# Recurrent slots, first down products and sixteen residual stores put in another order, in a decoder layer on one core

## The chip, the core and the metric

The kernel runs on one core of one Trainium2 chip. The core has TensorE (PE: matmuls, and PEld: the loads of their weights), VectorE (DVE), ScalarE (ACT), GpSimd (POOL), SyncE (SP, which here only gives out transfers) and 16 DMA engines that all transfers share. The metric is the device time of one execution in microseconds (us). Three runs of the kernel before took 1535.04, 1535.98 and 1536.03 us, so the median is 1535.98 us.

## The reference

One decoder layer over 1024 positions of 1024 channels in float32: RMSNorm, one input projection, two branches side by side, an output projection and a residual, and then an MLP with a residual and a last RMSNorm.

```python
h = rms_norm(x, g_mix)
z = h @ w_in + b_in                      # six parts: 1024, 1024, 1536, 1536, 1024, 1024 wide
# branch A: gated linear unit, causal width-31 depthwise conv, layer_norm, silu, @ w_a_out
# branch B: causal width-4 depthwise conv, then the gated recurrence:
r = sigmoid(block_diag(v, w_rg_a));  i = sigmoid(block_diag(v, w_rg_x))   # 16 heads of 96
a = exp(-8 * r * softplus(-lam));    h_t = a_t * h_{t-1} + sqrt(1 - a_t^2) * i_t * v_t
x = x + (sigmoid gates of both branches, merged) @ w_o
x = x + relu(rms_norm(x, g_mlp) @ w_1) ** 2 @ w_2
out = rms_norm(x, g_final)
```

## The kernel before

**Numbers.** A product in float32 is made of three products in a rounded format: each operand is split in a high and a low half, and high by high, high by low and low by high are added up in PSUM. So nearly every operand is followed by a split: ACT makes the high half by a copy, and the low half is the operand minus it. Either DVE subtracts (`low`, L1211), or ACT writes the negated high half, a POOL transfer adds the operand on top of it, and ACT copies (`split_dma`, L63 to L67). The large products (output projection, up and down projection) are block products of the Strassen kind, so that operands are sums of blocks (`d_sum`, L1866 to L1889) and results are added up block by block.

**Slots.** The input projection and the recurrence run as slots, `for s in range(3, NC1)` (L807 on). A slot is one 128-channel chunk of `z`, 48 matmuls (`chunk_mm(s, 0, 12)` and `chunk_mm(s, 12, 24)`, lines L723), with one head of the recurrence between or after them. A head has two products, one for each gate, of six matmuls (`head_mm`, L532 to L534), both in a PSUM bank that exists once. `head_gate` (sigmoid on ACT, L542) empties that bank. `head_mm(n, 0)` stands at the end of head n's slot and `head_mm(n, 1)` behind the first twelve pairs of the next one. Four heads make a group of three 128-channel tiles. One slot after a group's last head comes its `scan_exp` (L551 to L557: an exp and a tanh per tile on ACT), one more slot later its `scan_root`, and `scan_in` (the multiplication L462 of the gate `g` by the conv output `v`, on DVE) and `scan_tile` come in between. `EXP` maps these slots to the groups: {8: 0, 13: 1, 18: 2, 22: 3}. A tile `v` is made by an ACT pass and three conv taps (L474, L483), and `xb_parts` splits it into `vth` and `vtl` for the head (L488, with `split_dma`).

In these slots the order on every engine is written out. DVE's order is made by a small planner: `clk` holds an estimated time for each engine, `later(ready, cost, f)` puts work into a list with the time from which it can run, `vector_work(until)` gives that list out in order of those times and fills what is left of DVE's estimated time up to `until` with taps of the width-31 conv. `begun` is the planner's time for PE at the slot's start, `clk["P"]` its running time for PE.

**Output projection and residual.** The residual `x1` is made transposed (channels on partitions). `x1_turn` (L1528 on) turns half of it back with DVE transposes into four tiles `x1r` and stores each with four transfers into `x1d` in DRAM (L1539): 16 stores of 128 KB. These stand in the part in which SP's order too is written out. The other half goes through PE transposes (`x1_rows`, L1571). The down projection reads `x1d` back as `xb` (L2013).

**Up projection.** 104 steps (`useq`, L1942 on) of 12 matmuls each. Here the order on PE, ACT and DVE is written out. SP's and POOL's isn't: a scheduler places their transfers in the build. `UX` (L1843) maps a step number to additional calls.

**Down projection.** Four groups g of seven products p with two halves kk; `m` counts the 14 steps of a group (loop L2119 to L2165). In a step the operands of the next two steps are split (`left_high` on ACT L1904, `right` on ACT L1915; both return the low half as a function that is called later, DVE L1211), the block sums for later steps are made (`d_sum`), and two half products run on PE (`down_mm`, L1987). After the second half kk = 1 the results are taken over: the first half at once, the second (`down_add(g, p, 1)`) is held and given out at the start of the next step. For p = 1 that is an ACT copy `d0b<-d0a` (L2001), upon which p = 2 goes on adding in the bank `d0a`; for p = 2 it is a DVE addition into `xb` (L2005). In the steps called `joint` the low halves and the sums go out together after the first half product.

Tiles of [128, 1024] live in one pool of 37 buffers for the whole kernel, so a new tile can have to wait until a store of an old one has been read.

Of the kernel before, what the change touches and what calls it, by code (L numbers as in the profile page):

```python
# [15 lines left out]
P = 128  # L16
# [14 lines left out]
def trunk_kernel(ctx: ExitStack, tc: tile.TileContext, x, xt_in, xt_eo, vecs, w_in, w_a_out, w_b_pl, w_b_sq,  # L31
# [457 lines left out]
    def xb_parts(t):  # L489
        vp_[t] = T(f"vth{t}", F32R), T(f"vtl{t}", F32R)  # L490
        split_dma(vt[t], *vp_[t])
        parts[4 * (t // 3) + t % 3] = vp_[t]
        at("A", 2.1)
# [17 lines left out]
    def head_w(n):  # L511
        raw = rp.tile([HD, 2, HD], F32, tag="rraw", name=f"rraw{n}")
        nc.sync.dma_start(raw, w_rg[n])
        gws[n] = raw
# [33 lines left out]

    at_, rooted = {}, {}

    def scan_exp(g):  # L551
        at("A", 1.28)
        for t in range(3 * g, 3 * g + 3):
            r = gate[0, t]
            at_[t] = T(f"a{t}")
            nc.scalar.activation(at_[t], r, AF.Exp, scale=c8[:, t:t + 1])
            nc.scalar.activation(r, r, AF.Tanh, scale=c4[:, t:t + 1])  # L557
            at("A", 2.2)
# [8 lines left out]
    def scan_in(ready, *ts):  # L567
        for t in ts:
            later(ready, 1.2, nc.vector.tensor_tensor, gate[1, t], gate[1, t], vt.pop(t), ALU.mult)
# [144 lines left out]
    def chunk_mm(s, n0, n1, halves=(0, 1)):  # L714

        wh, wl = wst[s]
        if s not in zps:
            zps[s] = PS(f"z{s}")
        pairs = [x for k in range(8) for x in ((wh, k, 0), (wh, k, 1))] + [(wl, k, 0) for k in range(8)]
        for n in range(n0, n1):  # L720
            w, k, part = pairs[n]
            for hf in halves:
                nc.tensor.matmul(zps[s][:, HALVES[hf]], w[:, k, :], xw[k][part][hf],  # L723
                                 start=n == 0, stop=n == 23)
        at("P", len(halves) * (n1 - n0) * MM)
# [81 lines left out]
    with tc.manual_schedule(engines=ENGINES):  # L807
        for s in range(3, NC1):
            w_load(s + 2)
            for t in sorted(vp_):  # L810
                head_load(t)
            taps["hold"] = False
            begun = clk["P"]
            clk["A"], clk["V"] = max(clk["A"], begun + 0.5), max(clk["V"], begun - 2)

            if s == 3:

                chunk_mm(s, 0, 24, (1,))
                rs = first_scale()
                first_product(0, rs)  # L820
                xb_out(0, zps[0])
                first_parts(rs)
                chunk_mm(s, 0, 24, (0,))
            else:
                chunk_mm(s, 0, 12)
            before, new, nxt = (head_at.get(s + d) for d in (-1, 0, 1))
            if before is not None:

                head_gate(before, 0, begun)
                head_mm(before, 1)  # L830
            if made:
                xb_parts(made.pop())
            if s > 3:
                chunk_mm(s, 12, 24)
            if new is not None:
                head_mm(new, 0)

            c = CH[s - 1]
            if c >= XB:
                xb_out(c - XB, zps[s - 1])  # L840
            elif c >= GA:
                if CH[s] == c - GA + VA:
                    u_gate(c - GA, zps[s - 1])
                else:
                    u_out(c - GA, zps[s - 2], zps[s - 1])
            w_parts(s + 1)
            if before is not None:
                head_gate(before, 1, clk["P"] - 30 * MM)
            if s - 1 in EXP:

                scan_root(EXP[s - 1])
            if s == 3 or c >= XB:
                made.append(0 if s == 3 else c - XB)
            if nxt is not None:
                head_w_parts(nxt)
            if s == 5:
                decay_on()
            if s + 2 in head_at:
                head_w(head_at[s + 2])
            for d in range(5):  # L860
                if s - d in EXP:
                    g = EXP[s - d]
                    if d == 0:
                        scan_exp(g)
                        scan_in(begun + 3.5, 3 * g, 3 * g + 1)
                    elif d == 1:
                        scan_in(begun + 3.5, 3 * g + 2)

                    t = 3 * g + d - (2 if g < 3 else 1)
                    if 3 * g <= t < 3 * g + 3:  # L870
                        later(rooted[t], 4.8, scan_tile, t)
            if s == NC1 - 1:
                z_get(0, z_lhs)
                z_get(1, z_lhs)
            for f, *a in XS.get(s, ()):
                f(*a)
            if s == NC1 - 3:
                for i in range(4):
                    z_load(i // 2, i % 2)
            if s == 3:  # L880
                for c2 in range(4):
                    nc.sync.dma_start(xu[0, c2], xc[c2])
            vector_work(clk["P"] - 0.7)
# [646 lines left out]
    def x1_turn(kk):  # L1530
        for th in range(2):
            r = T(f"x1r{kk}{th}")
            for c2 in range(2):
                src = x1[kk, 0, c2].rearrange("p (m h b j) -> p h m b j", m=2, h=2, j=32)[:, th]
                dst = r.rearrange("p (b m j) -> p m b j", m=4, j=32)[:, 2 * c2:2 * c2 + 2]
                dve(0.65, 0, nc.vector.transpose, dst, src)
            d = x1d[2 * th:2 * th + 2].rearrange("q (b i) (k g x) -> k g i (q b) x", b=4, k=2, g=4)
            for g in range(4):
                nc.sync.dma_start(d[kk, g], r[32 * g:32 * g + 32].rearrange("p (b x) -> p b x", x=P))  # L1539

    def x1_cols():

# [271 lines left out]
    with tc.manual_schedule(engines=ENGINES):  # L1814
# [9 lines left out]
        for n in range(len(gseq) + 1):  # L1824
# [18 lines left out]
    UX = {0: ((g_parts, "u", 7, 0), (g_t, "u", 0, 4)), 1: ((g_parts, "u", 7, 1), (g_t, "u", 1, 4)),  # L1843
          2: ((g_parts, "u", 3, 0),), 3: ((g_parts, "u", 3, 1),), 4: ((g_parts, "u", 4, 0),),
          5: ((g_parts, "u", 4, 1),)}
    KC = 4
    NC_ = NP // KC
    BLK = {11: 0, 22: 1, 21: 2, 12: 3}
# [269 lines left out]
    with tc.manual_schedule(engines={mybir.EngineType.Activation, mybir.EngineType.DVE,  # L2118
                                     mybir.EngineType.PE}):  # L2119
        for n, (g, p, kk) in enumerate(dseq[:-2]):  # L2120
            m = n % 14
            end = g == NC_ - 1
            nx, nx2 = dseq[n + 1], dseq[n + 2]
            if m in DLOADS and not end:
                d_load(g + 1, *DLOADS[m])
            elif m == 0:
                d_load(g, *DFIRST)
            if n == 0:
                for q2 in range(2):
                    acc[0, 0, q2] = x_block(0, 0, q2)  # L2130
            if (g, m) in XADD:
                xbs[g, m] = x_block(*XADD[g, m])
            if held:
                held.pop()()
            lows_ = []
            if not end or m < 10:
                lows_.append(left_high(*nx))
            sums_ = d_sums(g, m)
            joint = not g and m in (2, 3)
            if sums_ and not joint:  # L2140
                d_sum(*sums_.pop(0))
            if not end or m < 10:
                lows_.append(right(*nx2))
            down_mm(g, p, kk, 0)
            if joint:
                for f in lows_:
                    f()
                for x in sums_[::-1]:
                    d_sum(*x)
            if kk:  # L2150
                if end and p == 7:
                    d_last(0)
                else:
                    down_add(g, p, 0)
            if not joint:
                for f in lows_:
                    f()
                for x in sums_:
                    d_sum(*x)
            if (g, m - 4) in XADD:  # L2160
                k = XADD[g, m - 4]
                tt(acc[k], acc[k], xbs.pop((g, m - 4)), ALU.add)
            down_mm(g, p, kk, 1)
            if kk:
                held = [lambda g=g, p=p: down_add(g, p, 1)]  # L2165
            if end:
                for f, *a in FX.get(m, ()):
                    f(*a)
        d_group(du["f", 0], z, 4, 0, (0, 1), False, True)
        d_last(1)  # L2170
        out_sq(1, 1, 0)
        out_sq(1, 1, 1)
        out_pre(1, 1, 1)
        close(0)
        d_group(du["f", 1], z, 4, P, (0, 1), False, True)
        closed(0)
        close(1)
        d_group(du["f", 2], z, 4, 2 * P, (0, 1), False, True)
        closed(1)
        close(2)  # L2180
        d_group(du["f", 3], z, 4, 3 * P, (0, 1), False, True)
        close(3)
        closed(2)
        closed(3)
# [80 lines left out]
```

## Time and profile before

| | |
|---|---|
| median of three runs | 1535.98 us |
| the profiled execution | 1536.15 us |
| its span, first to last instruction | 1534.1 us |
| outside the span | 2.05 us |
| granted TensorE clock, mean | 0.998 |
| busy: PE, DVE, ACT, POOL | 1521.0, 1199.6, 929.3, 192.3 us |
| HBM read, written | 149.79 MB, 60.82 MB |

The span is the time between the first and the last instruction of the profiled execution. A busy time is the sum of the engine's instructions. PE is busy for 99% of the span, so the kernel is a row of matmuls with few pauses, and 13.1 us lie in the pauses. In lists of single instructions the first column is the start in us from the span's begin, the second the duration, and brackets at the end give the idle time before it and what released it. Matmuls overlap in their pipeline: one of 128x512 shows as 0.39 us, yet the next one starts 0.23 us later.

### The profile page before, as it was taken

The numbers are of one execution on the slowest core, as the hardware profiler recorded it, in microseconds if no ns is written. First come the engines' busy times: TensorE is split into PE (matmuls) and PEld (weight loads), VectorE is DVE, ScalarE is ACT, GpSimd is POOL, SyncE is SP. The second block draws the span as 40 slices with busy tenths as digits, with TensorE's granted clock in tenths as the row PEclk, the third lists the DMA queues.
The fourth block names the chain that finished last, engine by engine and source line by source line (L and its number), as shares of the span: only waits on it lengthen the run. The fifth ranks groups of instructions, "written<-read, shape, count | busy, mean of one in ns | idle before, by whom it ended". The sixth has DMA issues, their size and how long they took to land.

```text
span 1534.1 us, 18971 instructions
## 1 busy us (share of the span) xinstructions
PE 1521.0 (99%) x6722; PEld 1250.4 (82%) x6722; DVE 1199.6 (78%) x1636; ACT 929.3 (61%) x1299; POOL 192.3 (13%) x228
## 2 busy tenths in 40 slices
PE   9999999999999999999999999999999999999998
PEld 7877877788888888888888887888888888888886
DVE  6989897899999997788769889755555386777777
ACT  6748678586566656735475877554444445545475
POOL 0111011012222222000022322000000000101010
PEclk9999999999999999999999999999999999999999
DMA  9766778898997889864779898333333974776465
GB/s 350 189 145 148 181 157 174 220 258 199 270 261 177 197 207 253 295 234 116 268 199 302 194 192 211 137 117 113 113 111 111 298 265 128 171 217 167 110 123 153
DMA packets 130799, 296.53 MB, mean 193 GB/s; under 512 B 12896, under 2 KB 34912, under 8 KB 130704
## 3 DMA queue, kind: packets, MB, share of 16 engines
q1 hardware_dynamic: 98960, 215.92, 41.9%
q0 software_dynamic: 31600, 79.15, 28.1%
q8 instruction: 52, 0.85, 0.2%
q14 instruction: 43, 0.35, 0.1%
q10 hardware_dynamic: 144, 0.26, 0.0%
HBM read 149.79 MB, written 60.82 MB: 137 GB/s over the span
## 4 chain that ended last, share of the span: by engine, by line
PE 86%; issue 5%; DVE 4%; DMA 3%; POOL 1%; ACT 1%; SPq 0%; POOLq 0%; DVEq 0%
PE z L723 12%; PE d1b L1987 2%; PE d2b L1987 2%; PE d0b L1987 2%; PE d3b L1987 2%; PE d0e L1987 1%; PE d3e L1987 1%; PE d3a L1987 1%; PE d2e L1987 1%; PE d2a L1987 1%; PE d1e L1987 1%; PE d1a L1987 1%; PE z L258 1%; DVE v L483 1%; DVE y L635 1%
## 5 line engine op out<-in xcount | busy, mean ns | idle before, releaser
L723 PE MATMUL z<-xh,win_h 128*128 128x512 f32 x368 | 115.4, 391 | 0.0
L723 PE MATMUL z<-xl,win_h 128*128 128x512 f32 x368 | 114.9, 390 | 0.0
L635 DVE SCALAR_TENSOR_TENSOR y<-u,vec,y 128x511 f32<-128x511 f32 (+14 forms) x120 | 88.5, 737 | 0.0
L723 PE MATMUL z<-xh,win_l 128*128 128x512 f32 x368 | 87.4, 389 | 0.0
L635 DVE SCALAR_TENSOR_TENSOR yt<-u,vec,yt 128x511 f32<-128x511 f32 (+6 forms) x112 | 82.6, 738 | 0.0
L635 DVE SCALAR_TENSOR_TENSOR y<-yt,csum,y 128x511 f32<-128x511 f32 (+6 forms) x112 | 82.6, 738 | 0.0
L723 PEld LDWEIGHTS z<-xh,win_h 128*128 128x128 f32 x368 | 69.1, 188 | 16.1 <-ACT win_h L67 0.5
L723 PEld LDWEIGHTS z<-xl,win_h 128*128 128x128 f32 x368 | 69.1, 188 | 15.0
L723 PEld LDWEIGHTS z<-xh,win_l 128*128 128x128 f32 x368 | 69.1, 188 | 14.5
L542 ACT ACTIVATE g<-rg,vec 96x1024 f32<-96x1024 f32 x32 | 35.5, 1110 | 65.3 <-PE rg L534 65.1
L1683 ACT ACTIVATE o<-s 128x512 fp32r<-128x512 f32 x56 | 33.7, 623 | 45.7 <-DVE s L1667 26.4
L66 POOL DMA_DIRECT2D zo<-zw x45 | 39.2, 871 | 134.4 <-ACT zo L65 122.8
L483 DVE SCALAR_TENSOR_TENSOR v<-xb,vec,v 128x1023 f32<-128x1023 f32 (+2 forms) x36 | 46.1, 1280 | 2.6 <-ACT v L474 1.8
L66 POOL DMA_DIRECT2D db_10l<-br x4 | 3.5, 876 | 340.5 <-ACT db_10l L65 340.5
L65 ACT ACTIVATE zo<-zw 128x512 fp32r<-128x512 f32 x45 | 28.2, 626 | 24.2 <-PE z2f L921 2.1
L66 POOL DMA_DIRECT2D win_l<-win_raw x23 | 20.0, 868 | 179.7 <-ACT win_l L65 151.1
L1211 DVE TENSOR_TENSOR o<-s,o 128x512 fp32r<-128x512 f32 x56 | 37.3, 684 | 1.4 <-ACT o L1683 1.4
L66 POOL DMA_DIRECT2D zo<-zs x30 | 26.4, 879 | 75.7 <-ACT zo L65 63.6
L462 DVE TENSOR_TENSOR g<-g,v 128x1024 f32<-128x1024 f32 x12 | 14.3, 1220 | 23.3 <-DMA g<-g 23.3
L67 ACT ACTIVATE zo<-zw 128x512 fp32r<-128x512 f32 x45 | 27.9, 621 | 0.0
L576 DVE TENSOR_TENSOR_SCAN g<-a,g 128x1024 f32<-128x1024 f32 x12 | 27.5, 2292 | 0.4
L66 POOL DMA_DIRECT2D ga<-gsa x8 | 7.0, 874 | 161.0 <-ACT ga L65 158.8
(3182 smaller groups left out, 4925.1 us busy)
## 6 DMA issues: line engine op xcount, KB each, us to landing
w_raw<-in_w_dram SPq DMA_DIRECT2D x34, 512.0 KB, 5.5
br<-in_w_dram SPq DMA_DIRECT2D x32, 512.0 KB, 5.9
ar<-fd SPq DMA_DIRECT2D x32, 512.0 KB, 6.9
zw<-in_w_in_dram SPq DMA_DIRECT2D x28, 512.0 KB, 6.9
win_raw<-in_w_in_dram SPq DMA_DIRECT2D x23, 512.0 KB, 5.0
win_l<-win_raw POOLq DMA_DIRECT2D x23, 512.0 KB, 5.1
zo<-zw POOLq DMA_DIRECT2D x45, 256.0 KB, 5.5
gates<-zg SPq DMA_DIRECT2D x32, 256.0 KB, 4.2
```

What stands on the lines that cost most here:

```text
L65: nc.scalar.activation(l, src, AF.Copy, scale=-1.0)
L66: nc.gpsimd.dma_start(l, src, accum_op=ALU.add)
L67: nc.scalar.activation(h, src, AF.Copy)
L258: nc.tensor.matmul(z0[i][:, HALVES[hf]], w0[i][w][:, k, :], xpart(a, hf, k), start=k == 0 and which == "hh", stop=k == 7 and which == ("hl ...
L483: nc.vector.scalar_tensor_tensor(v[:, d:S], a[:, 0:S - d], cbw_c[:, w * 12 + t:w * 12 + t + 1], v[:, d:S], ALU.mult, ALU.add)
L542: nc.scalar.activation(a, gps.pop((n, gi))[:HD, :], AF.Sigmoid, bias=(ba_c, bx_c)[gi][:, n:n + 1])
L576: nc.vector.tensor_tensor_scan(i, a, i, 0.0, ALU.mult, ALU.add)
L635: nc.vector.scalar_tensor_tensor(o[:, k:], a[:, 0:HS - k], c, o[:, k:], ALU.mult, add)
L723: nc.tensor.matmul(zps[s][:, HALVES[hf]], w[:, k, :], xw[k][part][hf], start=n == 0, stop=n == 23)
L1211: tt(l, src, h.bitcast(F32), ALU.subtract)
L1683: nc.scalar.activation(o[:, 0], src, AF.Copy)
L1987: nc.tensor.matmul(o, a, b, start=start and n == 0, stop=stop and n == len(todo) - 1, skip_group_check=not start or not stop)
```

## The change

There are three parts.

In the slots, `scan_exp` takes a function that it calls between the first tile and the second. The function gives out what DVE's list holds and splits a waiting `v` tile (`xb_parts`), if the slot begins no new head and a tile waits. That is so in slots 8 and 13. The slot that follows an `EXP` slot puts the previous head's second product behind 16 pairs instead of 12, which moves one in slot 19 only (slots 9, 14 and 23 follow slots that begin no head, so nothing stands between their two parts), and the planner's ready time for the second gate is adapted. `scan_in` goes out for all three tiles of a group at once: for the first three groups in the slot after, from its start on; for the last one in its own slot.

The 16 stores of `x1r` leave `x1_turn`. The tiles are kept in a list `turned`, and steps 8, 10, 12 and 14 of the up projection give out four stores each (`x1_rows_out`).

In the first group of the down projection step m = 4 becomes `joint` too, and in joint steps with kk = 0 (m = 2 and m = 4) the held `down_add` goes out behind the low halves instead of at the start of the step.

```diff
-    def scan_exp(g):
+    def scan_exp(g, f):
         at("A", 1.28)
         for t in range(3 * g, 3 * g + 3):
+            if t == 3 * g + 1:
+                f()
...
-                chunk_mm(s, 0, 12)
+                mid = 16 if s - 1 in EXP else 12
+                chunk_mm(s, 0, mid)
...
-                chunk_mm(s, 12, 24)
+                chunk_mm(s, mid, 24)
...
-                head_gate(before, 1, clk["P"] - 30 * MM)
+                head_gate(before, 1, clk["P"] - (2 * (24 - mid) + 6) * MM)
...
+            def parts_now():
+                if new is None and made:
+                    vector_work(0)
+                    xb_parts(made.pop())
...
                     if d == 0:
-                        scan_exp(g)
-                        scan_in(begun + 3.5, 3 * g, 3 * g + 1)
-                    elif d == 1:
-                        scan_in(begun + 3.5, 3 * g + 2)
+                        scan_exp(g, parts_now)
+                    if d == int(g < 3):
+                        scan_in(begun if d else clk["P"] - 2, 3 * g, 3 * g + 1, 3 * g + 2)
...
-            d = x1d[2 * th:2 * th + 2].rearrange("q (b i) (k g x) -> k g i (q b) x", b=4, k=2, g=4)
-            for g in range(4):
-                nc.sync.dma_start(d[kk, g], r[32 * g:32 * g + 32].rearrange("p (b x) -> p b x", x=P))
+            turned.append((kk, th, r))
+
+    turned = []
+
+    def x1_rows_out():
+        kk, th, r = turned.pop(0)
+        d = x1d[2 * th:2 * th + 2].rearrange("q (b i) (k g x) -> k g i (q b) x", b=4, k=2, g=4)
+        for g in range(4):
+            nc.sync.dma_start(d[kk, g], r[32 * g:32 * g + 32].rearrange("p (b x) -> p b x", x=P))
...
+    UX.update({n: ((x1_rows_out,),) for n in range(8, 16, 2)})
...
-            if held:
+            joint = not g and m in (2, 3, 4)
+            if held and not (joint and kk == 0):
                 held.pop()()
...
-            joint = not g and m in (2, 3)
...
             if joint:
                 for f in lows_:
                     f()
+                if held:
+                    held.pop()()
```

## The prediction

> **What bounds the kernel now.** I read the page's totals first, then the waits of PE, then PE's timeline at those waits, and then, at each, the engine that ends the wait. The totals:
>
> ```profile
> span 1534.1 us, 18971 instructions
> PE 1521.0 (99%) x6722; PEld 1250.4 (82%) x6722; DVE 1199.6 (78%) x1636; ACT 929.3 (61%) x1299; POOL 192.3 (13%) x228
> ```
>
> PE is the bound, and the change neither adds nor removes a matmul. So it can win only PE's pauses, and lose only by new ones. The waits of PE by releaser (us in total, times, longest):
>
> ```profile
> PE rg L534 <- DMA vtl<-v: 1.5, 1, 1.5
> PE rg L532 <- ACT g L542: 1.0, 3, 0.7
> PE d0b L1987 <- DVE da_61l L1211: 0.8, 1, 0.8
> PE f1d L1695 <- DMA o<-s: 0.4, 1, 0.4
> PE gu1a L1419 <- DMA gu<-w_raw: 0.2, 1, 0.2
> ```
>
> A pause costs more than its idle time, since the pipeline drains: a matmul is busy for 0.39 us, yet in a full stream the next starts 0.227 us later ((1.07 − 0.39)/3 in the first row below). PE's timeline at four of these places:
>
> ```profile
> 143.66 1.07 PE L723 MATMUL z<-xh,win_l 128*128 128x512 f32 x4
> 144.76 0.47 PE L532 MATMUL rg<-vth,rgh 96*96 96x512 f32 x1
> ...
> 197.17 0.40 PE L533 MATMUL rg<-vth,rgl 96*96 96x512 f32 x1
> 199.05 0.47 PE L534 MATMUL rg<-vtl,rgh 96*96 96x512 f32 x1 [1.49 <-DMA vtl<-v]
> ...
> 1248.08 0.39 PE L1987 MATMUL d0b<-db_61h,da_61h 128*128 128x512 f32 x1
> 1249.24 0.50 PE L1987 MATMUL d0b<-db_61h,da_61l 128*128 128x512 f32 x1 [0.77 <-DVE da_61l L1211]
> ```
>
> 199.05 − 197.17 − 0.23 = 1.65 us, where the wait says 1.5: add 0.16 to each wait. The matmul behind a pause is slower by some 0.09 (0.47 or 0.50 against 0.39). So a pause costs its idle time plus 0.25. The vtl wait costs 1.74, the three waits for a gate 1.0 + 3·0.25 = 1.75, d0b 1.04, f1d 0.64, gu1a 0.46. The pause at 144.76 has no idle time in the list: four matmuls from 143.66 end their places at 144.57, so it is 0.19 + 0.08 = 0.27. All together 5.9 us, 0.39% of the time: this is the most that the change can win.
>
> **Part A, the slots.** The engines that end those waits:
>
> ```profile
> 186.50 2.37 DVE L462 TENSOR_TENSOR g<-g,v 128x1024 f32<-128x1024 f32 x2 [5.96 <-DMA g<-g]
> 188.78 3.92 DVE L483 SCALAR_TENSOR_TENSOR v<-xb,vec,v 128x1023 f32<-128x1023 f32 x3
> ```
>
> ```profile
> 192.73 1.06 ACT L65 ACTIVATE vtl<-v 128x1024 fp32r<-128x1024 f32 x1 [2.50 <-DVE v L483]
> ...
> 204.75 1.11 ACT L542 ACTIVATE g<-rg,vec 96x1024 f32<-96x1024 f32 x1
> ...
> 263.58 1.06 ACT L67 ACTIVATE vth<-v 128x1024 fp32r<-128x1024 f32 x1 [0.23 <-PE rg L533]
> ...
> 266.44 1.10 ACT L542 ACTIVATE g<-rg,vec 96x1024 f32<-96x1024 f32 x1
> ```
>
> In slot 13 DVE stands idle for 5.96 us before `scan_in`, and the conv taps of v behind it come late for no reason of their own. ACT then waits 2.50 us for them, and the low half's transfer, begun after that, holds PE until 199.05. The new order flushes the taps ahead of `scan_in` and puts the split among the exps, so they run in those idle 5.96 us (180.5 to 186.5; the three need 3.92), and the split and its transfer begin more than 5 us sooner, against 1.65 that are wanted: the 1.74 go. ACT runs without a gap from 192.73 to past 205, so without the 2.50 the gates of head 8 come that much sooner: the pause before the first (0.4 by its share of the list) goes surely, that before the second (0.4) just about. In slot 8 the same order takes away a smaller wait of the same kind, and most likely the 0.27 at 144.76, the next gate but one.
>
> Slot 19: the biggest gate wait, 0.65 + 0.25 = 0.90. With 16 pairs instead of 12 ahead of it, eight more matmuls (8·0.227 = 1.8 us) cover it. But vth at 263.58 waits for a buffer that this head's own product reads (0.23 idle), so ACT slips by about 1 us, and the second gate, at 266.44 now, comes after PE wants it; I give half of the gain back, 0.45.
>
> `scan_in` in one go adds no instruction. DVE is idle for over a fifth of the span, and here for 5.96 us at a stretch, so a changed order of conv taps hides there; if it doesn't, a head's gate comes later by one 1.2 us operation, the lower end. SP gets the three `head_load` transfers a slot sooner and blocks at them until the split has landed; the weight load behind them isn't issued before the next slot's buffer comes free, so I take that as zero. A = −1.74 − 0.8 − 0.27 − 0.45 = −3.3. Bounds: −3.8 (all go) and −1.75 (vtl alone).
>
> **Part B, the stores.** SP's rows, the totals of three stretches (PE, PEld, DVE, ACT, POOL busy, clock, DMA share, GB/s), and for the transfer that f1d waits for POOL's issue, the matmul and the median of such transfers:
>
> ```profile
> 889.65 15.25 SPq L1539 DMA_DIRECT2D x1d<-x1r  x16
> 905.00 0.90 SPq L1650 DMA_DIRECT2D w_raw<-in_w_dram  x2
> ```
>
> ```profile
> 880.00:920.00 40.00, 40.00 (x203) 33.90 (x202) 32.06 (x57) 28.97 (x57) 12.22 (x14) 1.00 0.95 199
> 920.00:960.00 40.00, 39.41 (x177) 31.97 (x176) 37.68 (x52) 31.34 (x52) 10.55 (x12) 1.00 0.83 208
> 960.00:1000.00 40.00, 40.00 (x178) 33.14 (x177) 30.17 (x49) 23.15 (x35) 0.00 (x0) 1.00 0.39 135
> ```
>
> ```profile
> 943.52 0.87 POOL L66 DMA_DIRECT2D o<-s  x1 [0.96 <-ACT o L65]
> 951.92 0.50 PE L1695 MATMUL f1d<-gu7h,o 128*128 128x512 f32 x1 [0.38 <-DMA o<-s]
> o<-s POOLq DMA_DIRECT2D x8, 256.0 KB, 7.5
> ```
>
> Today the stores hold SP for 15.25 us, and the two weight loads behind them leave at 905.00 at the earliest. Each later stage of the weights (gu1a's transfer among them) hangs on such a load. Without the stores in front they can leave up to 15 us sooner, and the engines, 95% busy, have 2 MB less to move. Step 8 lies at about 959 us, where the share falls to 0.39: 16 issues of 0.95 us fit there beside a queue with little to do, and PE waits for none of them. gu1a's 0.46 goes. f1d's transfer took 951.92 − 943.52 = 8.4 us at most; 0.54 less (0.38 + 0.16) would do, and the median of its kind is 7.5, so with less traffic ahead I take its 0.64 too: B = −1.1. Bounds: 0 (the queue goes on as it is) and, upward, the third rival. The Trainium skill bears on this: DMA: Bandwidth & Descriptors, section "Issuing engines are not separate DMA queues", says that transfers end on the same 16 engines whoever gave them out; the 0.95 share beside SP's stores and POOL's slow transfers agrees. Its fit (section "Anatomy of one DMA — SWDGE (gpsimd) path"), 2.0 us plus bytes at 436 GB/s, would make 256 KB an estimated 2.6 us, and f1d's wait would be none at all; the measured 8.4 decides, and B would be the same by both, since I take that wait as gone.
>
> **Part C, the first down products.** ACT, PE and the chain of work, around 1232 us:
>
> ```profile
> 1231.96 1.01 ACT L2001 ACTIVATE d0b<-d0a 128x1024 f32<-128x1024 f32 x1 [0.42 <-PE d0a L1987]
> 1232.88 1.05 ACT L1904 ACTIVATE da_21h<-ar 128x1024 fp32r<-128x1024 f32 x1
> 1234.39 1.06 ACT L1915 ACTIVATE db_60h<-t 128x1024 fp32r<-128x1024 f32 x1 [0.46 <-DVE t L1885]
> ```
>
> ```profile
> 1234.48 0.39 PE L1987 MATMUL d0a<-db_20h,da_20h 128*128 128x512 f32 x1
> ```
>
> ```profile
> 1223.99 7.81 DMA fd<-fb
> ...
> 1233.14 1.22 DVE t L1885
> ...
> 1244.66 2.26 DVE xb L2005 x2
> 1246.92 0.93 DVE br L1887
> 1247.86 0.12 issue
> 1247.97 1.23 DVE da_61l L1211
> ```
>
> At m = 4 the low half da_61l now stands behind two additions and a sum. In the new order it comes behind the first addition alone, 2.2 us sooner (1.13 for the second, 1.05 for the sum and what lies behind it), and PE misses it by 0.93: the 1.04 goes.
>
> At m = 2 the same rule moves something else. What is held there is the ACT copy d0b<-d0a of the second half, which runs at 1231.96 today. It gets behind da_21h and db_60h. db_60h waits for the DVE sum t, which waits in DVE's order for a store fd<-fb that frees a buffer and takes 7.81 us. So db_60h still starts at 1234.39 and ends at 1235.45, and the copy ends at 1236.45. PE's product at 1234.48 adds in the very bank that the copy reads, and has to wait: 1236.45 − 1234.48 = 2.0, plus 0.1 for the slow start: +2.1. All later products come 2.1 us later, so da_61l's lateness would be gone anyway. C = −1.04 + 2.1 = +1.0. Bounds: −1.04 and +2.1 (if the store is slower still by 1 us, or m = 4 gains nothing).
>
> **Sum.** −3.3 − 1.1 + 1.0 = −3.4. On the profiled execution's 1536.15 that is 1532.75; that execution lies 0.17 above the median of the runs, so against 1535.98 I say 1532.6 us. About 0.2%, 3.1 us, is what a measurement of this kernel can tell from no change; the bound is 1532.9.
>
> **Rivals.** In each, what isn't named stays as forecast.
> *No new wait at m = 2.* The copy does no harm if db_60h ends by 1233.45, which needs the fd<-fb store landed by 1229.8, 5.8 us after its issue instead of 7.81. For it: the median of this kind is 3.4 us, below; against it: the chain above shows 7.81, and nothing in the change touches the traffic there.
>
> ```profile
> fd<-fb SPq DMA_DIRECT2D x16, 512.0 KB, 3.4
> ```
>
> Then −3.3 − 1.1 − 1.04 = −5.4: 1530.5.
> *The stores don't move.* SP's order isn't written out in the up projection, the tiles are ready at 889, and the scheduler may put them where they are now: −3.3 + 1.0 = −2.3: 1533.7.
> *The slots give only the vtl wait.* The ACT chain of slot 14 fills up again, or the second gate of slot 19 takes back all: −1.75 − 1.1 + 1.0 = −1.85: 1534.1.
> *Slower: the stores land beside the o<-s transfers*, around 943.52 in the 0.83 stretch, if the scheduler puts them in SP's gaps there. The 16 hold the queue for 15.25 us; four of them are 3.8 us of it, and eight, beside the two transfers that come last, 7.6, by which f1d and its successors come later. −3.3 + 1.0 + 7.6 = +5.3: 1541.3. It decides from about 5.4 us of lateness on (5.4 − 2.3 = 3.1). For it: the steps up there live on margins of a microsecond, as f1d's wait shows. Against: the four tiles go out two steps of 12 matmuls apart, 24·0.227 = 5.4 us of PE time, against the 3.8 that each takes. The same page's section "Queues, rings and completion order" says that an engine turns from one queue to the next packet by packet, by which POOL's transfers would get about half beside SP's; no row here separates the two.
>
> **How the numbers follow.** Forecast 0.38, no new wait 0.20, stores stay 0.16, slots give little 0.14, slower 0.12. The forecast is 0.3 us below the bound, so of its 0.38 I count 0.30 as faster and 0.08 as within; its own range is 1531.5 to 1533.8. Faster: 0.30 + 0.20 = 0.50. Within: 0.08 + 0.16 + 0.14 = 0.38. Slower: 0.12. The range runs from 1530.0, half a microsecond below the second case, to 1535.8, where A gives 1.75, B nothing and C costs 1.6, between its value and its upper end; only the slower case and some 0.07 of tails lie outside.
>
> **What would show it.** A: no vtl wait among PE's, no gate wait over 0.3, conv taps before `scan_in` on DVE in slot 13. B: SP's stores at 955 or later, w_raw ahead of 905, no waits of gu1a and f1d. C: PE's d0a product waits some 2 us for the ACT copy at 1234, and da_61l's wait is gone. Wrong would be: stores elsewhere in SP's order, or fd<-fb landing early, or a pause in the slots at a head that had none.

## The result, and the profile after

The median of 19 runs is 1532.90 us, against 1535.15 us for 19 runs of the kernel before: 2.25 us less. The ratio is 0.9986, with a 95% interval of 0.9979 to 0.9992, so the gain is between 1.2 and 3.2 us. That is faster, by less than the 0.2% that the prediction set as its bound. The profiled execution took 1532.83 us. Its span against that of before, from the pages' first lines:

```profile
span 1531.0 us, 18964 instructions
## 1 busy us (share of the span) xinstructions
PE 1519.7 (99%) x6722; PEld 1250.9 (82%) x6722; DVE 1200.4 (78%) x1636; ACT 928.2 (61%) x1299; POOL 192.3 (13%) x228
```

The span fell by 3.1 us. The runs say 2.25, because the one profiled execution of before (1536.15) lay a microsecond above the median of the 19 runs. PE's waits after the change, which answer to the five rows shown of before:

```profile
PE d0a L2002 <- ACT d0b L2016: 1.4, 1, 1.4
PE f0d L1709 <- DMA o<-s: 0.6, 1, 0.6
```

The waits in the slots, d0b's and f1d's are off the list, and gu1a's has become too short for it (0.1 us of idle time). There is a new one at d0a, and one of f1d's kind moved to f0d. PE's timeline at both (start, duration, what; in brackets the idle time before and its releaser):

```profile
944.48 0.39 PE L1709 MATMUL f0d<-gu7l,o 128*128 128x512 f32 x1
945.44 0.73 PE L1709 MATMUL f0d<-gu7h,o 128*128 128x512 f32 x2 [0.57 <-DMA o<-s]
...
1230.29 0.61 PE L2002 MATMUL d0a<-db_20l,da_20h 128*128 128x512 f32 x2
1232.35 0.50 PE L2002 MATMUL d0a<-db_20h,da_20h 128*128 128x512 f32 x1 [1.44 <-ACT d0b L2016]
```

Counted from start to start as in the prediction, with the slow matmul behind each pause: the slots' five pauses took 3.8 us before and nothing now. In the up projection gu1a and f1d cost 1.1 before, gu1a and f0d 1.2 now. In the down projection d0b cost 1.05 before; d0a costs 1232.35 − 1230.52 − 0.23 + 0.11 = 1.7 now. That is −3.8 + 0.1 + 0.7 = −3.0, against 3.1 of span: the account closes, and says that in these two profiles one part of the change did all the good.

The order in slot 13, DVE and then ACT: the taps run at 177.00 and not at 188.78, and the split stands among the exps.

```profile
177.00 3.92 DVE L483 SCALAR_TENSOR_TENSOR v<-xb,vec,v 128x1023 f32<-128x1023 f32 x3 [0.64 <-ACT v L474]
...
186.16 3.50 DVE L462 TENSOR_TENSOR g<-g,v 128x1024 f32<-128x1024 f32 x3
```

```profile
185.35 1.04 ACT L65 ACTIVATE vtl<-v 128x1024 fp32r<-128x1024 f32 x1
```

SP's rows around the stores, and POOL's issue for gu1a after and, in the last fence, before:

```profile
885.84 1.35 SPq L1553 DMA_DIRECT2D x1d<-x1r  x3
887.29 1.55 SPq L1664 DMA_DIRECT2D w_raw<-in_w_dram  x1
888.89 0.62 SPq L1553 DMA_DIRECT2D x1d<-x1r  x1
889.91 0.35 SPq L1664 DMA_DIRECT2D w_raw<-in_w_dram  x1
890.37 12.65 SPq L1553 DMA_DIRECT2D x1d<-x1r  x12
```

```profile
917.20 0.95 POOL L66 DMA_DIRECT2D gu<-w_raw  x1 [5.91 <-ACT gu L65]
```

```profile
921.02 0.95 POOL L66 DMA_DIRECT2D gu<-w_raw  x1 [5.91 <-ACT gu L65]
```

The stores begin at 885.84, against 889.65 before. That is 3.8 us earlier, just what the slots gave, so they didn't move at all. Only two weight loads slipped in among them. gu1a's transfer leaves at 917.20, against 921.02, again 3.8 earlier and no more: it waits for ACT, whose order is written out, and not for those loads.

### The profile page after: what moved, and what is told of

Read it like the earlier page. It is cut to its first block, busy times and chain, and to the rows that moved or that the text cites. A ratio compares the mean times of both kernels' runs of the same rounds, so it can differ in the third digit from the quotient of the medians.

```text
span 1531.0 us, 18964 instructions
## 1 busy us (share of the span) xinstructions
PE 1519.7 (99%) x6722; PEld 1250.9 (82%) x6722; DVE 1200.4 (78%) x1636; ACT 928.2 (61%) x1299; POOL 192.3 (13%) x228
## 4 chain that ended last, share of the span: by engine, by line
PE 95%; issue 2%; DMA 1%; DVE 1%; ACT 1%; POOL 1%; SPq 0%; POOLq 0%; DVEq 0%; ACTq 0%
PE z L725 16%; PE z L258 2%; PE d2b L2002 2%; PE d1b L2002 2%; PE d0b L2002 2%; PE d3b L2002 2%; PE d0e L2002 1%; PE d3a L2002 1%; PE d2e L2002 1%; PE d2a L2002 1%; PE d1e L2002 1%; PE d1a L2002 1%; PE d3e L2002 1%; PE rg L532 1%; PE rg L534 1%
## 5 line engine op out<-in xcount | busy, mean ns | idle before, releaser
L1219 DVE TENSOR_TENSOR o<-w_raw,o 128x512 fp32r<-128x512 f32 x38 | 25.9, 684 | 0.0
```

What stands on the lines that cost most here:

```text
L1219: tt(l, src, h.bitcast(F32), ALU.subtract)
```

## The experiments

**Each part alone.** Three kernels, each the kernel before with one of the three parts of the diff (the slots, the stores, the down products).

> The slots' part alone (scan_exp, mid, scan_in). Theory: all five pauses of PE in the slots of the recurrence go, 3.8 us against before, and PE's timeline shows no pause over 0.3 us from 100 to 300; the waits of gu1a, f1d and d0b stay as before. Rival (the prediction's sum): half of slot 19's pause comes back at the second gate, 3.3 us. Rival: a part of the gain is lost later, because a chain that is bound by transfers doesn't come earlier with it: under 2.5 us.

> The stores' part alone. Theory: SP still issues the sixteen stores at 889 to 905, with two weight loads among them instead of behind them, and since POOL's gu transfers wait for ACT's written order and not for those loads, nothing changes: within 0.3 us of before, gu1a and f1d wait as before by 0.2 and 0.4 us of idle time, or f0d in its place by as much. Rival (the prediction): loads that leave up to 15 us sooner take gu1a's and f1d's pauses away, 1.1 us faster. Rival: stores and loads together are slower, 0.5 us or more slower.

> The down projection's part alone. Theory: d0b's pause at 1248 (1.05 us) goes and PE gets a pause of 1.7 us before its d0a product at 1234, released by the ACT copy: 0.7 us slower. Prediction: 1.0 us slower. Rival: without the shift from the slots the fd<-fb store lands soon enough and there is no new pause: 1.0 us faster.

| part | median us | before | ratio, 95% interval |
|---|---|---|---|
| slots | 1532.29 | 1535.51 | 0.9980 (0.9972 to 0.9989) |
| stores | 1535.08 | 1535.51 | 0.9999 (0.9990 to 1.0008) |
| down products | 1536.59 | 1535.51 | 1.0007 (0.9998 to 1.0016) |

The slots' part gives 3.2 us, and its trace has no pause in the slots. The stores' part is no difference that can be measured. The down products cost 1.1 us by the medians; the interval takes in zero by a hair, but the trace has the new pause and no wait at d0b any more:

```profile
PE d0a L1987 <- ACT d0b L2001: 1.5, 2, 1.2
```

The 1.2 is the held copy's; the other 0.3 comes from the copy of the first half. The three parts sum up to −2.6, where the whole change gave −2.25. So nothing here says that the parts act on each other, though with intervals of about ±1.3 us a microsecond of it would not be seen. In the kernel with the stores' part alone POOL's issue for gu1a and the waits at f1d read:

```profile
920.86 0.95 POOL L66 DMA_DIRECT2D gu<-w_raw  x1 [5.90 <-ACT gu L65]
```

```profile
PE f1d L1701 <- DMA o<-s: 0.5, 1, 0.5
PE f0d L1701 <- DMA o<-s: 0.2, 1, 0.2
```

The first weight load left 14 us sooner (890.95 against 905.00), and gu1a's transfer 0.16 us. The waits for o<-s are no smaller. gu1a's is off this list, by no more than it varies between kernels that don't touch it (see the last section).

**The held copy.** Two kernels treat m = 2 in another way. The first leaves the copy where it was and defers at m = 4 only:

```diff
-            if held and not (joint and kk == 0):
+            if held and not (joint and m == 4):
```

> The whole change, but the held copy is deferred at m = 4 only and stays first at m = 2. Theory: the pause at d0a goes and d0b's doesn't come back: 1.7 us faster than the whole change, 4.8 us faster than before. Rival: DVE's chain around 1232 to 1250 sets the end there, so that da_61l comes late again once PE is 1.7 us earlier: only 0.7 us faster than the whole change.

It took 1531.64 us against 1535.51, ratio 0.9975 (0.9964 to 0.9985). That is 3.9 us below before, where 4.8 was expected, and 1.3 us below the whole change by the medians, with intervals of the two ratios that overlap slightly. By the spans it is 1.6 (1529.4 against 1531.0). Neither d0a nor d0b is in the list of its waits. So the rival's mechanism, that DVE makes da_61l late again, did not happen.

The second is the kernel before with the down part alone, but with the copy one place earlier on ACT at m = 2, behind da_21h and ahead of db_60h:

```diff
             if not end or m < 10:
                 lows_.append(left_high(*nx))
...
+            if held and m == 2:
+                held.pop()()
             if not end or m < 10:
                 lows_.append(right(*nx2))
```

> The down projection's part with one step between: at m = 2 the held copy stands behind da_21h on ACT, but ahead of db_60h. Theory: the pause at d0a comes from the copy standing behind db_60h, which waits for the sum behind the store; one place earlier the copy ends by about 1234, and the pause at d0a is at most 0.3 us, that at d0b gone: 0.8 to 1.1 us faster than before by the pauses. Rival: any deferral behind ACT's next operand costs it, and the pause stays over 1 us.

ACT's rows, of the whole change first, and then of this kernel:

```profile
1230.32 1.06 ACT L1930 ACTIVATE db_60h<-t 128x1024 fp32r<-128x1024 f32 x1 [1.81 <-DVE t L1900]
1231.29 1.01 ACT L2016 ACTIVATE d0b<-d0a 128x1024 f32<-128x1024 f32 x1
```

```profile
1230.80 1.04 ACT L1904 ACTIVATE da_21h<-ar 128x1024 fp32r<-128x1024 f32 x1
1231.74 1.00 ACT L2001 ACTIVATE d0b<-d0a 128x1024 f32<-128x1024 f32 x1
1233.61 1.06 ACT L1915 ACTIVATE db_60h<-t 128x1024 fp32r<-128x1024 f32 x1 [0.87 <-DVE t L1885]
```

In the change the copy stands ready and waits 1.81 us behind an operand that isn't. One place earlier it has ended by 1232.74, and PE has neither pause, at d0a nor at d0b. So it isn't the deferral that costs, but what the copy was put behind. (Of time there is one run, 1534.11 us beside 1534.13 of before, too few for a gain of one microsecond.)

**What in the slots does it.** Three kernels, each the slots' part without one of its edits: 12 pairs instead of 16, no split among the exps, and `scan_in` as before.

> The slots' part with 12 pairs ahead of the second head product everywhere, so the split among the exps and scan_in in one go without the move of a product. Theory: the 16 pairs in slot 19 aren't what removes its pause of 0.8 us: the gate of head 12 ends at about 258.4, as DVE no longer holds the exps, and a product 1.8 us sooner would want it at 258.4; a pause of at most 0.3 us is left in slot 19, the other four places stay without. Rival (the prediction's step): only the cover of eight matmuls removes it, and the pause is back with 0.8 us or more.

> The slots' part without the split among the exps: scan_in in one go in the slot after, and 16 pairs. Theory: scan_in's move alone takes the conv taps out from behind the wait for the transferred gates, so ACT has no wait of 2.5 us, the low half leaves 1.2 to 2.5 us sooner and the vtl pause shrinks from 1.7 to 0.5 us or less; the gate pauses at 205 and 212 go. Rival (the prediction's step): it takes the split among the exps, and the vtl pause stays with 1.5 us or more.

> The slots' part with scan_in as before: split among the exps, and 16 pairs. Theory: the flush puts the conv taps ahead of scan_in, so the pauses at 197, 205 and 212 are gone as in the whole part; in slot 18, which flushes nothing, the exp still waits for DVE's scan_in, and what is left is at slot 19, 0.5 us or less thanks to the 16 pairs. Rival: scan_in's new place is what matters, and the vtl pause is back with 1.5 us.

Single runs gave 1531.86, 1532.12 and 1532.15 us beside 1534.13 of before. With 12 pairs PE's second product of head 12 comes 1.6 us sooner than in the change (258.60 against 260.20), and finds the bank as good as free (ACT's gate, then PE):

```profile
257.43 1.11 ACT L542 ACTIVATE g<-rg,vec 96x1024 f32<-96x1024 f32 x1
```

```profile
258.12 0.61 PE L725 MATMUL z<-xl,win_h 128*128 128x512 f32 x2
258.60 0.48 PE L532 MATMUL rg<-vth,rgh 96*96 96x512 f32 x1
```

The gate comes 3.5 us sooner than before (260.97), while PE wants it 2.8 sooner (258.57 against 261.33, by the end of the matmuls ahead). The 0.8 us pause of slot 19 was this difference; eight matmuls aren't needed to cover it. What had made the gate late before is ACT's last exp ahead of it, which waited for `scan_in` on DVE; in the whole change it doesn't, and the gate follows (before, then after):

```profile
257.32 1.15 ACT L556 ACTIVATE a<-g,c 128x1024 f32<-128x1024 f32 x1 [0.68 <-DVE g L462]
...
260.97 1.11 ACT L542 ACTIVATE g<-rg,vec 96x1024 f32<-96x1024 f32 x1
```

```profile
257.24 1.11 ACT L542 ACTIVATE g<-rg,vec 96x1024 f32<-96x1024 f32 x1
```

Five profiles have the slots as before: that of before, the stores alone, the down products alone, the stores by ACT below, and the kernel with the copy between. In them this exp waited 0.68, 0.27, 0.15, 0.37 us and not at all, and PE's idle time in slot 19 was 0.65, 0.25, 0.13, 0.35 us and none. The pause follows the wait for `scan_in`, and before is the one in which it was longest. Without the split among the exps the low half leaves 2.7 us sooner than before (194.09) all the same, and that is enough (POOL's issue before and in this kernel, then PE's product):

```profile
194.09 0.87 POOL L66 DMA_DIRECT2D vtl<-v  x1 [13.77 <-ACT vtl L65]
```

```profile
191.35 0.87 POOL L66 DMA_DIRECT2D vtl<-v  x1 [11.16 <-ACT vtl L65]
```

```profile
197.04 0.39 PE L533 MATMUL rg<-vth,rgl 96*96 96x512 f32 x1
197.26 0.40 PE L534 MATMUL rg<-vtl,rgh 96*96 96x512 f32 x1
```

So either edit alone takes the 1.7 us away: `scan_in` in the next slot takes the taps out from behind the wait, and the flush puts them ahead of it. With the old `scan_in` a pause in slot 19 stays, at the second gate and 0.6 us long, not the 0.5 or less that was expected: ACT's split, which stands ahead of that gate, is released by a conv tap on DVE, most likely over a buffer of the common pool (PE's wait, then ACT):

```profile
PE rg L532 <- ACT g L542: 0.5, 1, 0.5
```

```profile
261.93 1.06 ACT L67 ACTIVATE vth<-v 128x1024 fp32r<-128x1024 f32 x1 [2.44 <-DVE y L637]
```

**Stores that really come late.** The kernel before with `x1_rows_out`, but given out by ACT, whose order is written out in the up projection:

```diff
-            nc.sync.dma_start(d[kk, g], ...)
+            nc.scalar.dma_start(d[kk, g], ...)
```

> The kernel before with the sixteen stores given out at steps 8, 10, 12 and 14 of the up projection by ACT instead of SP; ACT's order is written out there, so they really come late, near 955 to 980. Theory: with 2 MB less to move from 889 to 905 POOL's gu transfers land sooner and gu1a's pause (0.4 us) goes, f0d's and f1d's (together 0.5 to 1.1 us in the kernels so far) lie ahead of the stores and stay: 0.3 to 0.6 us faster. Prediction, had the stores moved: 1.1 us faster. Rival: the stores hold up the o<-s and the weights of the steps beside them, or ACT by their issue: new pauses of PE from 955 to 990, 1 us slower or more.

The stores now leave from 963.3 to 978.9. It took 1534.84 us against 1535.74, ratio 0.9996 (0.9987 to 1.0004): no difference that the runs can tell. The trace shows two pauses less and two more. First the stretch 880 to 920 (the DMA share is the last but one column) and the transfers issued from 920 to 960, then the same transfers in the kernel before:

```profile
880.00:920.00 40.00, 40.00 (x203) 33.87 (x201) 31.98 (x56) 28.98 (x57) 12.21 (x14) 1.00 0.78 154
```

```profile
o<-s POOLq DMA_DIRECT2D x7, 256.0 KB, 4.2
```

```profile
o<-s POOLq DMA_DIRECT2D x7, 256.0 KB, 6.9
```

With the stores out of the way the share falls from 0.95 to 0.78 in this stretch, the o<-s of the next one land in 4.2 us in place of 6.9, and the waits of gu1a and f1d are gone. Against the expectation f1d's goes too: three weight loads of SP that left beside its transfer before, at 942.58, now leave at 948.47. That a transfer given out by POOL is faster when SP has fewer in flight fits the Trainium skill, DMA: Bandwidth & Descriptors, section "Issuing engines are not separate DMA queues", by which transfers of all engines interleave on the same 16. But two new pauses come:

```profile
PE f2c L1701 <- DVE fa L1727: 0.4, 1, 0.4
PE f0d L1701 <- DVE gu4l L1211: 0.3, 1, 0.3
```

**The best of it.** The slots' part with the m = 4 deferral, with the stores as before; the same with the stores by ACT at steps 8 to 14; the same at steps 16, 20, 24 and 28.

> The slots' part and the down projection's part with the held copy deferred at m = 4 only; the stores as before. Theory: the stores' part is worth nothing, so this is as fast as the whole change with the copy left at the start of m = 2: 3.9 to 4.8 us faster than before. Rival: the stores' part helps once the other pauses are gone, and this is 0.5 us or more slower than that kernel.

> The same with the sixteen stores given out by ACT in the up projection. Theory: 0.3 to 0.6 us faster than with the stores as before, by gu1a's pause. Rival: the late stores cost as much in the steps beside them: no difference or slower.

> The best kernel so far (slots' part, held copy deferred at m = 4 only, stores by ACT), with the stores at steps 16, 20, 24 and 28 instead of 8, 10, 12 and 14. Theory: the one pause left there, f2c's 0.6 us, comes from four ACT issues in steps that ACT and DVE fill anyway, so with single stores further apart it goes and no pause of PE over 0.3 us is left from 940 to 1100: 0.6 us faster than that kernel. Rival: the tiles held for longer keep buffers from the weights, and a new wait takes its place: no faster.

| kernel | median us | ratio to before, 95% interval |
|---|---|---|
| stores as before | 1531.65 | 0.9970 (0.9958 to 0.9981) |
| stores by ACT, from step 8 | 1530.94 | 0.9965 (0.9952 to 0.9979) |
| stores by ACT, from step 16 | 1531.47 | 0.9973 (0.9962 to 0.9984) |

The first has the time of the kernel with m = 2 left alone, so the stores' part is worth nothing there too. The second has the lowest median of all, 1530.94 us, some 2 us below the whole change; its runs went from 1530.74 to 1531.30 and overlap a little with the first's. That the late stores give these 0.7 us isn't shown. In the profiles PE has one wait each behind the first 40 us: f2c's 0.4 in the second, and in the first none in the up projection, but one at d0a:

```profile
PE d0a L1995 <- ACT d0b L2009: 0.7, 1, 0.7
```

```profile
1216.28 9.07 DMA fd<-fa
```

It belongs to the copy of the first half, which no edit moved: it came late behind da_20h, which waited for a store that took 9.07 us. The kernel with m = 2 left alone has no such pause, with the same code there. The third missed what was expected: f2c's pause stays, and ends at 969.6, ahead of its first store at 979.7. So ACT's issues aren't its cause. SP's weight loads show another, first with the stores as before, then by ACT from step 8, with DVE's wait for them there:

```profile
938.82 6.64 SPq L1658 DMA_DIRECT2D w_raw<-in_w_dram  x3
```

```profile
945.18 8.28 SPq L1664 DMA_DIRECT2D w_raw<-in_w_dram  x3
```

```profile
951.90 0.69 DVE L1680 TENSOR_TENSOR s<-w_raw 128x512 f32<-128x512 f32 x1 [0.98 <-DMA w_raw<-in_w_dram]
```

These loads leave 6.4 us later. With the stores as before, the o<-s issued from 932 to 938, ahead of the loads, land in 3.9 us by the median, and those from 938 to 944, beside them, in 7.5; by ACT it is 3.5 and 4.4. So what slows the o<-s is likely these loads and not the stores 40 us earlier; no run moved the loads alone. The delay also makes DVE wait 0.98 us for them, after which it runs about a microsecond late up to f2c, which is the loss. That they are late because the tiles of the stores hold their buffers is likely, since nothing else was changed, but no run took a buffer away to show it.

## Why the prediction was right, and where it wasn't

The forecast was 3.4 us less, and the measured gain is 2.25 by the runs and 3.1 by the spans. The time lay within the range. That it came within 0.3 us of the forecast 1532.6 is luck: the three runs of before that it started from have a median 0.8 us above that of 19 runs, and from 1535.15 the same sum would have given 1531.75, 1.15 too low. By the runs of the single parts the slots and the down products came within 0.1 us of their terms (with intervals of about ±1.3 us), and the stores' term is what was missing. In the profiles the slots gave 0.5 more and the down products cost 0.3 less than forecast, which hid most of it. Point by point:

- **Slots, −3.3 forecast, −3.8 in the trace, −3.2 by the runs of the part alone.** The wait for vtl, the gates of head 8 and the small pause in slot 8 went as worked out. The step that failed is slot 19: "the second gate ... comes after PE wants it; I give half of the gain back". ACT doesn't slip there. Before, its exp at 257.32 waited 0.68 us for DVE's `scan_in`; in the change the gate ends by 258.35 and the split follows at once. The eight matmuls that were counted as the cover aren't needed at all. The second gate does come too late where `scan_in` stays as it was. The mechanism of the vtl wait was right, but each of two edits would have done. The term itself was read from one profile: for the same matmuls from 130 to 300 us PE took 3.8 us longer before than with the slots' part, but only 3.0 to 3.4 in the four other profiles with the slots as before, which agrees with the 3.2 of the runs.
- **Stores, −1.1 forecast, 0.1 slower in the trace, nothing by the runs.** This is the step that was wrong. "Step 8 lies at about 959 us" took the place in the code for the place in SP's order, and the rival that the stores don't move is what happened. The second half failed too: "Each later stage of the weights (gu1a's transfer among them) hangs on such a load". The loads did leave 12 to 14 us sooner, and gu1a's transfer left when ACT let it. When the stores were really made late, the gain that was forecast at gu1a and f1d came, and about as much was lost again at f0d and f2c, which no step had counted.
- **Down products, +1.0 forecast, +0.7 in the trace, +1.1 by the runs of the part alone.** Both halves were right: d0b's pause went, and PE waited for the ACT copy behind db_60h. The term that was mis-sized is the new wait, 2.1 forecast and 1.7 measured. The chain after the change shows the store that it hangs on at 7.49 us, where 7.81 was taken:

```profile
1220.25 7.49 DMA fd<-fb
...
1230.32 1.06 ACT db_60h L1930
1231.38 0.92 ACT d0b L2016
```

- **The rivals.** Of the four, "the stores don't move" came true; its gain of 2.3 us is the measured 2.25, and its 1533.7 lies above 1532.90 only by the base it was counted from. In the profiles the slots gave more than it took over from the forecast, and d0a's wait was less. No new wait at m = 2 and little from the slots did not happen. The slower one found no occasion, since the stores never came near the o<-s transfers.
- **The chances.** Half of the weight was on faster by over 0.2%; the measured gain is 0.14%. The sum was made on one execution of before that lay high, which made the pauses to be won in the slots look longer than in the other profiles, and a bound only 0.3 us away from a forecast with terms of 1 us wasn't worth half of the chances on one side.

## What to carry to other kernels

Where one queue's order is written out and another's is left to a scheduler, a line that is moved in the code may move nothing in the second, as the sixteen stores here: read in the trace what the scheduler did with ready work before, and pin a transfer to an engine with a written order if its place matters. When work is put off for the sake of one engine, look at what it lands behind on its own: a copy that was ready cost PE 1.7 us because it was put behind an operand that wasn't, and one place earlier it had no pause behind it. And before counting the cover that an edit brings, ask if the wait isn't already gone by the edit next to it.

## What wasn't expected

Pauses that hang on a transfer scatter from kernel to kernel where no edit touched them. gu1a's idle time, of kernels with the same order there, was 0.3 us in the slots' part, 0.6 with the old `scan_in`, and not in the list in the kernel with 12 pairs:

```profile
PE gu1a L1427 <- DMA gu<-w_raw: 0.3, 1, 0.3
```

```profile
PE gu1a L1428 <- DMA gu<-w_raw: 0.6, 1, 0.6
```

d0b's idle time was 0.8 us before and 0.2 in the kernel with the stores' part alone, which doesn't touch it. Each kernel was profiled once, so it stays open how much of this is between kernels and how much between executions of one. Either way a pause of half a microsecond in one profile isn't a safe price, and the stores' term of the forecast was made of two of these.
